# A hybrid RWKV-7 and short-convolution layer on one core: new layouts for values and decays, one more buffer for the inverse, PSUM banks shared out differently, output weights loaded in steps

## The chip, the cores and the metric

The kernel runs on one core of one Trainium2 chip, as one program. The core has five engines with their own instruction queues: TensorE (PE in the profile; PEld is its loading of weights), VectorE (DVE), ScalarE (ACT), GpSimd (POOL) and SyncE (SP), which here does nothing but issue DMAs. The metric is the device time of one execution in microseconds (us); lower is better. Three runs of the kernel before took 1731.84, 1737.47 and 1740.01 us, so its time is given as the median, 1737.47 us.

## The reference

One inference step of a one-layer backbone over 128 context tokens and 2048 latent tokens of width 1024. Cut to what matters:

```python
h = rmsnorm(x) * (1 + scale) + shift            # scale, shift from c @ w_ada
r, k, v, g_a, b_gate, c_gate, u, g_b = split(h @ w_in)      # 8 x 512 columns
r, k, v = token_shift(r, k, v)                  # mix with both neighbours
w = exp(-exp(-softplus(-(w0 + tanh(h @ dd) @ du)) - 0.5))   # decay, per direction
a = sigmoid(ib + (h @ idn) @ iu)                            # per direction
# per direction and head (8 heads of 64), over the tokens in scan order:
S = S * w_t - (S kk_t) (kk_t * a_t)^T + v_t k_t^T ;  y_t = S r_t
ya = (groupnorm(y_fwd + y_bwd) * gn_w + gn_b + bonus * v) * silu(g_a)
yb = b_gate * conv3(c_gate * u) * silu(g_b)
out = rmsnorm(x + gate * (concat(ya, yb) @ w_out)) * final_g
```

The context is scanned from a zero state and its final states are an output; the latent scans start from cached states.

## The kernel before

All data are float32, and products that need the precision are made from a high and a low part. There are three phases, written as Python generators that are advanced in turns. Between phases data pass through scratch tensors in HBM (`S[...]`, shapes in `SCR`, L686).

**Phase 1** (`phase1`, L49) works on blocks of 384 tokens (`BLK`, six of them, the last 256) in three thirds of two blocks. For each of four head pairs `g` it runs `mixA` (keys, receptance, decays, rates; L350) for both blocks of the third and then `gateA` (values and gate; L424), with the convolution group (`convB`, `gateB`) between. `dense` (L153) makes each projection from 24 matmuls.
- In `mixA`, for each direction `d`, `pt` holds exp of the cumulated log decay of each chunk of 64 tokens. It has one buffer for each direction (`NPP = 1`, L296). One element for each chunk, the whole chunk's decay, is stored by a DMA that ScalarE issues (L404): 48 DMAs, with a row of 6 (or 4) separate elements for each of 128 partitions. Phase 2 loads them as `B.pc` (L764).
- In `gateA`, `vt` holds the transposed, mean-free values with tokens on the partitions, and one DMA of SP stores it (L444) to `S["vt"]`, which is (token, 512). In the first third `vt` has one buffer under the tag "vt", which the low parts `hsl...` of `part_sum` (L200, L195, subtraction on POOL at L197) use too.

**Phase 2** (`phase2`, L704) works on 17 stages; 16 of them hold 8 chunks of one head pair in both directions, and stage 15 holds the context. The parts of a stage are: `partL` loads operands, `partM` makes within-chunk matrices F, GA and Q on TensorE (L905, L898; PSUM pool `pm` with 2 banks, L718) and sends the small diagonal blocks to HBM, `partI` inverts these on POOL (L932 to L948; tile `zt` with 2 buffers), `partW`, `partU` and `partB` load and combine, and `partS` (L1047) does the scan: 8 steps, in each step two heads' matmuls for each of the two directions into `psS` (PSUM pool `pS`, 4 banks, L752), then the next state from `psS` on VectorE (L1080). One `psS` tile holds four steps of one direction. After the fourth, `outputs` (L1088) takes it out of PSUM: a copy on ScalarE for the direction that comes first to a block of tokens (L1099, done at L792), an add on VectorE (L1097) for the other. `load_v` (L832) loads the values into `sv`: for each of 64 partitions 8 pieces of 128 elements; for the context in two DMAs.

The parts run ahead of one another: in stage s the scan of s is interleaved with `partM` of s + 3, and with `partW`, `partU` and `partB` of s + 1, by the strings `ORDER` and `MORD`. What is emitted in this order is then laid out by the framework's scheduler (`schedule_with_timeline_sim=True`, L1422), which orders each engine's instructions by its own model of times; each engine then works strictly through its list. So the order on an engine is close to, but not, the order of the source.

**Phase 3** (`phase3`, L1265) is the output projection, 17 tiles of 128 tokens. From stage 14 on phase 2's pools `pm`, `r2` and `r1` are closed and `weights` (L1306) loads the four blocks of output weights for the convolution half (`load_k`, L1276: a DMA, a copy on ScalarE to the high part, a subtraction on VectorE to the low part; `raw` has 2 buffers), all before the scan of stage 14 is emitted. `ahead` (L1314) then makes the convolution half of three tiles, a half tile for each step of the scan; `tail` does the rest after stage 16.

Of the kernel before, what the change touches and what calls it, by code (L numbers as in the profile page):

```python
# [6 lines left out]
F32 = mybir.dt.float32  # L7
F32R = mybir.dt.float32r
# [3 lines left out]
PSUM = bass.MemoryType.PSUM  # L12
DRAM = bass.MemoryType.DRAM

NT = 2176
# [33 lines left out]
def phase1(K):  # L49
# [285 lines left out]

    npair = [0]
# [13 lines left out]
    def mixA(g, j, ws, hh, lw, pre):  # L350

        t0, n = BLK[j]
        nch = n // 64
        tl = lambda tag, b=1: (tp if tag == "sg" else ta_).tile([128, 384], F32, tag=tag, name=f"{tag}_{g}_{j}_{K.u()}", bufs=b)
# [16 lines left out]
        for d in range(2):  # L371
# [32 lines left out]
            nc.scalar.dma_start(S[f"pc{d}"][g * 128:(g + 1) * 128, t0 // 64:t0 // 64 + nch], pt[:, :nch, 64 - 64 * d])  # L404
# [10 lines left out]
            kds.append(kd)  # L415
        bs = kds[0]
# [7 lines left out]
    def gateA(g, j, ws, hh, bsum):  # L424

        t0, n = BLK[j]
        tl = lambda tag, b=1: (tp if tag == "sg" else ta_).tile([128, 384], F32, tag=tag, name=f"{tag}_{g}_{j}_{K.u()}", bufs=b)
# [16 lines left out]
        nc.sync.dma_start(S["vt"][t0:t0 + n, g * 128:(g + 1) * 128].rearrange("(a p) c -> p a c", p=128), vt[:, :n // 128])  # L444
# [241 lines left out]
SCR = {}  # L686
for _d in range(2):
    SCR[f"ops{_d}"] = (4, 512, NT)
    SCR[f"pc{_d}"] = (512, 34)
SCR.update(vt=(NT, 512), sg=(512, NT), q=(512, NT), mixT=(1024, NT))  # L690
# [13 lines left out]
def phase2(K):  # L704
# [8 lines left out]
    def setup_first():  # L713
# [4 lines left out]
        O.pm = Pool(K, "p2m", "right", 2, PSUM)  # L718
# [29 lines left out]
    def setup_rest():  # L748
# [3 lines left out]
        O.pS = Pool(K, "p2S", "left", 4, PSUM)  # L752
# [10 lines left out]
        for d in range(2):  # L763
            D(B.pc[:, d], S[f"pc{d}"].rearrange("(e c) n -> c e n", c=64))  # L764
# [67 lines left out]
    def load_v(dst, units):  # L832
        if units[0][0] == units[-1][0]:
            p, c0 = units[0]
            D(dst.rearrange("t u h v -> t u (h v)"), S["vt"][c0 * 64:(c0 + 8) * 64, p * 128:(p + 1) * 128].rearrange("(u t) c -> t u c", t=64))
        else:
            for u in range(2):
                D(dst.rearrange("t (g u) h v -> t u g (h v)", u=2)[:, u], S["vt"][u * 64:u * 64 + 64, :].rearrange("t (g c) -> t g c", g=4))
# [83 lines left out]
    def partI(s, st):  # L922
# [5 lines left out]
        zt = tl([128, 16, 32], "zt", 2, O.rI)  # L928
# [336 lines left out]
def phase3(K):  # L1265
# [10 lines left out]
    def load_k(k, hi, lo, eng):  # L1276

        raw = O.r.tile([128, 1024], F32, tag="raw", name=f"woraw{k}", bufs=2)
        D(raw[:], A["wout"][k * 128:(k + 1) * 128, :])
        P.copy(hi[:], raw[:])  # L1280
# [25 lines left out]
    def weights():  # L1306
# [3 lines left out]
        for k in CONV:  # L1310
            load_k(k, *[O.r.tile([128, 1024], F32R, name=f"wo{a}{k}") for a in "hl"], V)
        z0[AHEAD[0]] = O.r.tile([128, 1024], F32, name="z0_0")

    def ahead():  # L1314
        for i in AHEAD:
# [111 lines left out]
```

## Time and profile before

| | |
|---|---|
| median of 3 runs | 1737.47 us (1731.84 to 1740.01) |
| the profiled execution | 1726.64 us, of which the span from first to last instruction is 1724.9 us |
| instructions | 32848 |
| stages of phase 2 by the first and last scan matmul | stage 0 from 1017.3 us, stage 14 from 1456.1, stage 15 from 1480.0, stage 16 from 1528.4 to 1561.0 us |
| mean granted TensorE clock | 0.970 |

The profiled execution is 10.8 us, or 0.6%, shorter than the median. In the rows, "PE psF L905 <- ACT Q L792: 9.4, 17, 1.6" reads: the matmuls of line 905 that write tile psF waited for the instruction of ScalarE that writes Q, 9.4 us in total, 17 times, at longest 1.6 us. A row of a timeline has the start and the duration in us, the engine, the line, the operation, output <- inputs with their shapes, how many instructions are merged in the row, and in brackets the engine's idle time before it with what ended it. A row of the windows view has, for each engine, its busy time and its number of instructions, then the granted TensorE clock (1.00 is full), the DMA engines' busy share and GB/s.

### The profile page before, as it was taken

The page shows a single profiled execution, that of the slowest core. Times are in us where ns is not written, and L with a number is a line of the kernel's source. Part 1 is how long each engine was busy: PE and PEld are TensorE (multiplying, and loading weights), DVE is VectorE, ACT ScalarE, POOL GpSimd, SP SyncE. Part 2 cuts the span into 40 slices and gives each one's busy share as a digit, 9 for nine tenths or more (in the row PEclk, how much of TensorE's full clock was granted, in tenths as well). Part 3 has the DMA queues.
Part 4 walks back from the last instruction along what each step waited for, and adds up shares of the span by engine and source line. Part 5 has one row for each costly group of instructions (what it writes and reads, how often), then busy time and mean ns, then how long its engine had stood idle before and what let it go on. Part 6 is the DMA issues. An engine that isn't in the chain of part 4 may idle for free. (4 is left out here: it accounts for less than half of the span.)

```text
span 1724.9 us, 32848 instructions
## 1 busy us (share of the span) xinstructions
PE 1640.9 (95%) x12400; PEld 1556.2 (90%) x12400; DVE 1107.3 (64%) x2092; ACT 868.8 (50%) x1719; POOL 587.4 (34%) x1089
## 2 busy tenths in 40 slices
PE   5989899999999999999999989999999999999998
PEld 2889889899999999999999989999999999887886
DVE  5875778775568858587854344666766656646433
ACT  4533454443243534244423187788878777643222
POOL 0010111111110201021213737877877768223221
PEclk8899999999999999999999999899999989899999
DMA  9687778675557657567896376677878874746442
GB/s 372 212 221 235 223 245 252 199 234 183 173 182 209 176 173 188 167 188 248 208 304 218 112 191 154 163 185 186 203 186 189 189 177 106 195 153 202 147 147 92
DMA packets 314286, 335.66 MB, mean 195 GB/s; under 512 B 165448, under 2 KB 262344, under 8 KB 300048
## 3 DMA queue, kind: packets, MB, share of 16 engines
q1 hardware_dynamic: 277184, 328.97, 65.3%
q10 hardware_dynamic: 35584, 0.14, 1.3%
q0 software_dynamic: 1360, 4.46, 0.7%
q8 instruction: 98, 1.61, 0.4%
q14 instruction: 60, 0.49, 0.1%
HBM read 221.42 MB, written 112.08 MB: 193 GB/s over the span
## 5 line engine op out<-in xcount | busy, mean ns | idle before, releaser
L947 POOL TENSOR_TENSOR zt<-zt,ztmp 128x30 f32<-128x30 f32 (+7 forms) x510 | 198.6, 389 | 39.3
L1067 PE MATMUL psS<-sv,E 128*128 128x64 f32 x1088 | 154.4, 277 | 0.0
L1067 PEld LDWEIGHTS psS<-sv,E 128*128 128x128 f32 x1088 | 145.4, 200 | 1.9
L1042 PE MATMUL psE<-str,stl 128*128 128x128 f32 x1088 | 140.8, 278 | 5.4 <-DVE E L1043 3.8
L944 POOL TENSOR_TENSOR ztmp<-ab,zt 128x60 f32<-128x60 f32 (+7 forms) x255 | 133.5, 524 | 19.4
L1042 PEld LDWEIGHTS psE<-str,stl 128*128 128x128 f32 x1088 | 129.8, 192 | 7.1 <-DVE E L1043 4.8
L323 POOL TENSOR_TENSOR shk<-rawl 128x384 f32<-128x384 f32 (+1 forms) x24 | 23.0, 959 | 322.6 <-ACT rawl L319 322.6
L1080 DVE TENSOR_TENSOR sv<-psS,pc 64x128 f32<-64x128 f32 x254 | 69.4, 277 | 97.3 <-PE psS L1067 96.9
L792 ACT COPY bd<-rr 64x512 f32<-64x512 f32 x136 | 84.0, 617 | 77.2 <-issue 24.5
L1043 DVE TENSOR_TENSOR E<-psE,msk 128x512 f32<-128x512 f32 x136 | 92.9, 685 | 27.6 <-PE psE L1042 26.9
L905 PE MATMUL psF<-rr,bd 128*128 128x128 f32 x544 | 78.8, 291 | 13.0 <-ACT Q L792 10.6
L1363 POOL TENSOR_TENSOR z<-z,x 128x512 f32<-128x512 f32 x32 | 43.6, 1364 | 126.5 <-DVE z L1359 105.8
L905 PEld LDWEIGHTS psF<-rr,bd 128*128 128x128 f32 x544 | 69.2, 199 | 16.3 <-ACT Q L792 13.1
L1031 PE MATMUL psX<-F,zb 128*128 128x128 f32 x544 | 80.7, 303 | 2.7 <-ACT zb L790 1.7
L323 POOL TENSOR_TENSOR shv<-rawl 128x384 f32<-128x384 f32 (+1 forms) x24 | 22.3, 930 | 178.2 <-ACT rawl L319 172.9
L905 PE MATMUL psG<-rr,bd 128*128 128x128 f32 x544 | 74.8, 286 | 2.9 <-DVE F L906 2.9
L1031 PEld LDWEIGHTS psX<-F,zb 128*128 128x128 f32 x544 | 73.7, 214 | 3.6 <-ACT zb L790 2.4
L160 PE MATMUL mmc<-h,w 128*128 128x384 f32 (+1 forms) x192 | 66.7, 347 | 6.8 <-ACT ta L397 3.4
L905 PEld LDWEIGHTS psG<-rr,bd 128*128 128x128 f32 x544 | 68.2, 199 | 3.3 <-DVE F L906 3.0
L161 PE MATMUL mmc<-h,w 128*128 128x384 f32 (+1 forms) x192 | 65.5, 341 | 0.0
L162 PE MATMUL mmc<-h,w 128*128 128x384 f32 (+1 forms) x192 | 65.4, 340 | 0.0
L160 PE MATMUL mmgb<-h,w 128*128 128x384 f32 (+1 forms) x192 | 64.4, 335 | 0.4 <-ACT q1r L321 0.4
(307 smaller groups left out, 5177.2 us busy)
## 6 DMA issues: line engine op xcount, KB each, us to landing
w<-scr_wsp SPq DMA_DIRECT2D x68, 1024.0 KB, 6.7
scr_wsp<-w SPq DMA_DIRECT2D x34, 1024.0 KB, 9.0
rr<-scr_ops SPq DMA_DIRECT2D x64, 512.0 KB, 4.4
scr_ops<-pair SPq DMA_DIRECT2D x80, 384.0 KB, 6.7
wr<-in_win SPq DMA_DIRECT2D x34, 512.0 KB, 6.1
ab<-scr_at SPq DMA_DIRECT2D x34, 256.0 KB, 3.8
x<-in_x SPq DMA_DIRECT2D x17, 512.0 KB, 3.7
wadas<-in_wada SPq DMA_DIRECT2D x8, 1024.0 KB, 14.1
```

The lines of the kernel that those rows point to most:

```text
L160: T.matmul(ps[:, :n], w[:, 0, k], hh[:, 0, k, :n], start=k == 0, stop=False)
L161: T.matmul(ps[:, :n], w[:, 0, k], hh[:, 1, k, :n], start=False, stop=False)
L162: T.matmul(ps[:, :n], w[:, 1, k], hh[:, 0, k, :n], start=False, stop=k == 7)
L792: (V.tensor_copy if k in ON_DVE else P.copy)(dst, src)
L905: T.matmul(ps[:, i, :].rearrange("p (a b) -> p a b", b=64), w[:, u, :], x[:, :, u, :], start=True, stop=True)
L944: G.tensor_tensor(tv, ab[:, j:j + 2, j + 2:32].unsqueeze(1).broadcast_to((128, kn, 2, n)), zt[:, :kn, j:j + 2].unsqueeze(3).broadcast_to(( ...
L947: G.tensor_tensor(zt[:, :kn, j + 2:32], zt[:, :kn, j + 2:32], tv[:, :, r], ALU.subtract)
L1031: T.matmul(px[:, i, :], B.zb[:, gi, us.start + i, :], g.F[:, us.start + i, :], start=True, stop=True)
L1042: T.matmul(pe[:, i, hd, :].rearrange("p (b t) -> p b t", b=2), g.lt[:, :, hd, us.start + k + i].rearrange("p b t -> p (b t)"), g.rt[:, :, ...
L1043: V.tensor_tensor(g.E[n][:, k:k + 2].rearrange("p a b c -> p (a b) c"), pe[:].rearrange("p a b c -> p (a b) c"), B.msk[:, ME[g.d]].unsquee ...
L1067: T.matmul(sp[gi][:, q, hd, :], g.E[n][:, k, hd, :], sv[:, u, hd, :], start=True, stop=True)
L1080: r = V.tensor_tensor(dst, sp[gi][0:64, q], B.pc[0:64, d, 2 * p:2 * p + 2, c:c + 1].broadcast_to((64, 2, 64)), ALU.mult)
```

## The change

Five edits:
- The values' scratch tensor becomes (4 head pairs, 64 tokens, 34 chunks, 128). A store becomes two DMAs, one for the even and one for the odd chunks, each from 64 partitions; a load takes 8 chunks that lie together (one piece of 1024 elements for each partition), and the context's load becomes one DMA.
- The chunk decays of both directions and both blocks of a third are gathered by a POOL copy into a tile `pcs`, and stored by one DMA of SP after the second block: 12 DMAs instead of 48 of ScalarE.
- `zt` gets a third buffer.
- PSUM pool `pm` gets 3 banks in place of 2 and `pS` 3 in place of 4.
- `weights` only starts the loading of the first two weight blocks. The copies and subtractions, and the loading of the other two, become steps of `ahead`, one block at each step of the scan, so that the convolution halves come five steps later.

```diff
@@ -333,6 +333,7 @@
         t0, n = BLK[j]
         nc.sync.dma_start(S[name][g * 128:(g + 1) * 128, t0:t0 + n], t_[:, :n])
 
+    pcsum = {}
     npair = [0]
 
     def pair():
@@ -351,6 +352,10 @@
 
         t0, n = BLK[j]
         nch = n // 64
+        c0, pc0 = t0 // 64, BLK[j - j % 2][0] // 64
+        if j % 2 == 0:
+            pcsum[g] = tp.tile([128, 2, 12], F32, tag="pcs", name=f"pcs{g}_{j}", bufs=2)
+        pcs = pcsum[g]
         tl = lambda tag, b=1: (tp if tag == "sg" else ta_).tile([128, 384], F32, tag=tag, name=f"{tag}_{g}_{j}_{K.u()}", bufs=b)
         wk, wr_ = ws
         psk, psr = pre or (None, None)
@@ -401,7 +406,7 @@
             V.tensor_tensor(v3(al), v3(kk), pt[:, :nch, d:64 + d], ALU.mult)
             V.tensor_tensor(v3(rh), v3(rS), pt[:, :nch, 1 - d:65 - d], ALU.mult)
             spill2(d, 2 * d, g, j, ar)
-            nc.scalar.dma_start(S[f"pc{d}"][g * 128:(g + 1) * 128, t0 // 64:t0 // 64 + nch], pt[:, :nch, 64 - 64 * d])
+            G.tensor_copy(pcs[:, d, c0 - pc0:c0 - pc0 + nch], pt[:, :nch, 64 - 64 * d])
 
             kd = tl("kd", 2)
             P.activation(kd[:, :n], ta[:, :n], AF.Identity, bias=dcol(D_KA2 + g), scale=vcol(V_KA + g))
@@ -413,6 +418,8 @@
             V.tensor_tensor(be[:, :n], be[:, :n], c[:, :n], ALU.mult)
             spill2(d, 2 - 2 * d, g, j, kb)
             kds.append(kd)
+        if j % 2:
+            nc.sync.dma_start(S["pc"][g * 128:(g + 1) * 128, :, pc0:c0 + nch], pcs[:, :, :c0 + nch - pc0])
         bs = kds[0]
         V.tensor_tensor(bs[:, :n], kds[0][:, :n], kds[1][:, :n], ALU.add)
         V.scalar_tensor_tensor(bs[:, :n], bs[:, :n], dcol(D_RKQ + g), rS[:, :n], ALU.mult, ALU.mult)
@@ -424,6 +431,7 @@
     def gateA(g, j, ws, hh, bsum):
 
         t0, n = BLK[j]
+        nch = n // 64
         tl = lambda tag, b=1: (tp if tag == "sg" else ta_).tile([128, 384], F32, tag=tag, name=f"{tag}_{g}_{j}_{K.u()}", bufs=b)
         wv, wg = ws
         vS = shifted(dense(wv, hh, n, "v"), j, 2, g, "v", 1)
@@ -441,7 +449,8 @@
         mn = ta_.tile([128, 3, 2], F32, tag="vmean", name=f"vmean{g}_{j}", bufs=1)
         V.tensor_reduce(mn[:, :m], heads(psv), mybir.AxisListType.X, ALU.add)
         V.scalar_tensor_tensor(heads(vt), mn[:, :m].unsqueeze(3).broadcast_to((128, m, 2, 64)), -1.0 / 64, heads(psv), ALU.mult, ALU.add)
-        nc.sync.dma_start(S["vt"][t0:t0 + n, g * 128:(g + 1) * 128].rearrange("(a p) c -> p a c", p=128), vt[:, :n // 128])
+        for i in range(2):
+            nc.sync.dma_start(S["vt"][g, :, t0 // 64 + i:t0 // 64 + nch:2], vt[i * 64:i * 64 + 64, :nch // 2])
 
         psg = dense(wg, hh, n, "g")
         tg = tl("sg", 2)
@@ -686,8 +695,7 @@
 SCR = {}
 for _d in range(2):
     SCR[f"ops{_d}"] = (4, 512, NT)
-    SCR[f"pc{_d}"] = (512, 34)
-SCR.update(vt=(NT, 512), sg=(512, NT), q=(512, NT), mixT=(1024, NT))
+SCR.update(pc=(512, 2, 34), vt=(4, 64, 34, 128), sg=(512, NT), q=(512, NT), mixT=(1024, NT))
 
 
 
@@ -715,7 +723,7 @@
         O.r0 = Pool(K, "p2r0", "right")
         O.rI = Pool(K, "p2rI", "right")
         O.r1 = Pool(K, "p2r1", "right")
-        O.pm = Pool(K, "p2m", "right", 2, PSUM)
+        O.pm = Pool(K, "p2m", "right", 3, PSUM)
         B.msk = O.r0.tile([128, 4, 128], F32, name="msk")
         B.mkg = O.r0.tile([128, 2, 128], F32, name="mkg")
         for i, j in enumerate((0, 2, 4, 5)):
@@ -749,7 +757,7 @@
         O.l0 = Pool(K, "p2l0", "left")
         O.l1 = Pool(K, "p2l1", "left")
         O.p2 = Pool(K, "p2s", "left", 2, PSUM)
-        O.pS = Pool(K, "p2S", "left", 4, PSUM)
+        O.pS = Pool(K, "p2S", "left", 3, PSUM)
         O.r2 = Pool(K, "p2r2", "right")
         new_slot(O.r2)
         cp = O.l0
@@ -761,7 +769,7 @@
         V.memset(B.geps[:], 64e-5)
         B.pc = cp.tile([64, 2, 8, 34], F32, name="pc")
         for d in range(2):
-            D(B.pc[:, d], S[f"pc{d}"].rearrange("(e c) n -> c e n", c=64))
+            D(B.pc[:, d], S["pc"][:, d].rearrange("(e c) n -> c e n", c=64))
 
         lt = ring(O.l1, 2, [128, 2, 8, 128], "stl", lambda t_: presetS(vl(t_)))
         rt = ring(O.l1, 2, [128, 2, 2, 8, 64], "str", presetS)
@@ -832,10 +840,9 @@
     def load_v(dst, units):
         if units[0][0] == units[-1][0]:
             p, c0 = units[0]
-            D(dst.rearrange("t u h v -> t u (h v)"), S["vt"][c0 * 64:(c0 + 8) * 64, p * 128:(p + 1) * 128].rearrange("(u t) c -> t u c", t=64))
+            D(dst.rearrange("t u h v -> t u (h v)"), S["vt"][p, :, c0:c0 + 8])
         else:
-            for u in range(2):
-                D(dst.rearrange("t (g u) h v -> t u g (h v)", u=2)[:, u], S["vt"][u * 64:u * 64 + 64, :].rearrange("t (g c) -> t g c", g=4))
+            D(dst.rearrange("t (g u) h v -> t g (u h v)", u=2), S["vt"][:, :, 0:2].rearrange("g t u c -> t g (u c)"))
 
     H0, H1, FULL = slice(0, 64), slice(64, 128), slice(0, 128)
 
@@ -925,7 +932,7 @@
         ab = tl([128, 32, 32], "ab", 2, O.rI)
         for h in range(2):
             D(ab[h * 64:h * 64 + 64].rearrange("p j i -> p (j i)"), at.rearrange("u s b j i -> (u s b) (j i)"))
-        zt = tl([128, 16, 32], "zt", 2, O.rI)
+        zt = tl([128, 16, 32], "zt", 3, O.rI)
         zf = zt[:].rearrange("p a b -> p (a b)")
         tmp = tl([128, 512], "ztmp", 1, O.rI)
         dg = tl([128, 16], "dgp", 1, O.rI)
@@ -1273,10 +1280,15 @@
     AHEAD = TILES[:3]
     z0 = {}
 
-    def load_k(k, hi, lo, eng):
+    def load_raw(k):
 
         raw = O.r.tile([128, 1024], F32, tag="raw", name=f"woraw{k}", bufs=2)
         D(raw[:], A["wout"][k * 128:(k + 1) * 128, :])
+        return raw
+
+    def load_k(k, hi, lo, eng, raw=None):
+
+        raw = raw or load_raw(k)
         P.copy(hi[:], raw[:])
         eng.tensor_tensor(lo[:], raw[:], hi[:].bitcast(F32), ALU.subtract)
         wk[k] = (hi, lo)
@@ -1307,11 +1319,16 @@
         O.r = Pool(K, "p3r", "right")
         O.pr = Pool(K, "p3pr", "right", 2, PSUM)
         O.pu = O.pr
-        for k in CONV:
-            load_k(k, *[O.r.tile([128, 1024], F32R, name=f"wo{a}{k}") for a in "hl"], V)
+        O.raw = [load_raw(k) for k in CONV[:2]]
         z0[AHEAD[0]] = O.r.tile([128, 1024], F32, name="z0_0")
 
     def ahead():
+        yield
+        for n, k in enumerate(CONV):
+            load_k(k, *[O.r.tile([128, 1024], F32R, name=f"wo{a}{k}") for a in "hl"], V, O.raw[n])
+            if n < 2:
+                O.raw.append(load_raw(CONV[n + 2]))
+            yield
         for i in AHEAD:
             ms = load_m(O.r, i, CONV, 1)
             if i not in z0:
```

## The prediction

> **What bounds the kernel now.** I read the page first, then a windows view cut at the phases, then TensorE's waits by stretch, and last timelines around single waits.
>
> ```profile
> PE 1640.9 (95%) x12400; PEld 1556.2 (90%) x12400; DVE 1107.3 (64%) x2092; ACT 868.8 (50%) x1719; POOL 587.4 (34%) x1089
> ```
>
> TensorE is busy for 95% of the span, and no other engine comes near. An edit here is worth what it takes from TensorE's idle time or gives to it, and idle time of other engines does not count by itself. Where the idle time lies (columns: us, then busy us and instructions of PE, PEld, DVE, ACT, POOL, then clock, DMA share, GB/s):
>
> ```profile
> 0.00:150.00 150.00, 122.86 (x627) 103.09 (x627) 106.69 (x209) 62.82 (x118) 11.79 (x25) 0.92 0.81 261
> 150.00:975.00 825.00, 802.82 (x4841) 789.17 (x4840) 573.89 (x1042) 334.63 (x677) 151.46 (x201) 0.99 0.70 208
> 975.00:1017.00 42.00, 34.83 (x347) 33.05 (x346) 16.38 (x34) 22.95 (x46) 14.26 (x29) 0.88 0.64 154
> 1017.00:1476.00 459.00, 445.24 (x5322) 434.19 (x5320) 284.84 (x588) 362.96 (x696) 350.78 (x786) 0.96 0.71 171
> 1476.00:1528.00 52.00, 47.55 (x395) 42.28 (x395) 29.90 (x56) 32.55 (x58) 10.80 (x15) 0.90 0.71 193
> ```
>
> TensorE is idle for 27 us in the start-up, which no edit touches; 22 us in the rest of phase 1; 7 us between the phases; 14 us in fifteen stages of the scan; and 4.5 us where the output weights come in. There is a second loss: a clock of 0.96 over 459 us is 18 us of work. Its form is stretches at half clock, such as these two; the row of TensorE is the wait right ahead of the second:
>
> ```profile
> 1378.55 1.82 PE L905 MATMUL psF<-rr,bd 128*128 128x128 f32 x8 [1.63 <-ACT Q L792]
> 1099.00:1109.20 10.20, 10.20 (x100) 9.73 (x101) 1.72 (x5) 3.99 (x7) 6.42 (x17) 0.50 0.41 126
> 1378.90:1389.10 10.20, 10.20 (x103) 9.73 (x102) 2.88 (x6) 4.28 (x8) 7.71 (x19) 0.50 0.64 174
> ```
>
> So what all edits together could win at most is about 22 + 7 + 14 + 4.5 = 48 us of idle time and 18 us of clock. What TensorE waited for in phase 1, and then in the scan, says how much of that they reach:
>
> ```profile
> PE pss L204 <- ACT hshs L196: 5.5, 3, 3.0
> PE pss L205 <- POOL hsls L197: 3.3, 2, 2.6
> PE mmc L160 <- ACT q1r L321: 2.9, 4, 2.0
> PE psq L205 <- POOL hslq L197: 1.7, 1, 1.7
> ```
>
> ```profile
> PE psF L905 <- ACT Q L792: 9.4, 17, 1.6
> PE psW L1012 <- ACT bu L792: 1.5, 4, 0.5
> ```
>
> **Decays in 12 stores.** Removed are 48 issues on ScalarE; added are 48 copies on POOL, which I price by the nearest row, POOL's copy of 128x16, and 12 issues on SP, priced like a value store below.
>
> ```profile
> L404 ACTq DMA_DIRECT2D scr_pc<-pp x48: 366/366/1160, 80.9 to 864.9; - x48
> 1202.12 0.21 POOL L936 COPY dgp<-ab 128x16 f32<-128x16 f32 x1
> q10 hardware_dynamic: 35584, 0.14, 1.3%
> ```
>
> ScalarE gets back 48 x 0.366 = 17.6 us in phase 1. It is busy for 335 of 825 us there, and what delays TensorE through it (5.5 + 2.9 us above) are instructions that ScalarE itself got late from VectorE. At best all 8.4 us go; I take 1. POOL gets 48 x 0.21 = 10 us, and is busy for 151 of 825 us. The copy waits for the exp of `pt`. What is queued behind it on POOL are the shift additions and the low parts, and these wait for ScalarE instructions that stand behind that exp anyway. So the wait adds nothing and the copy lies in idle time; without that cover TensorE, which waits for POOL's low parts, pays 0.21 us at each of the 3 places above, under 1 us. The 35584 packets of 4 bytes that go were 1.3% of the DMA engines' span; loads of weights gain a little, which the rows don't carry to TensorE. Term: -1 us (-8.4 to +1).
>
> **Values by head pair.** There are 24 more stores on SP, and lighter loads.
>
> ```profile
> L444 SPq DMA_DIRECT2D scr_vt<-vt x24: 359/371/1010, 131.7 to 885.6; - x24
> POOL hslq L197 <- DMA scr_vt<-vt: 25.8, 2, 16.4
> scr_vt<-vt SPq DMA_DIRECT2D x20, 192.0 KB, 4.1
> sv<-scr_vt SPq DMA_DIRECT2D x32, 256.0 KB, 4.0
> ```
>
> The issues cost SP 24 x 0.37 = 9 us and the decay stores 12 x 0.37 = 4.4 us, spread over 750 us; queued behind them are loads and stores that wait for engines anyway. The landing matters in the first third, where the low parts use the same buffer: POOL waited 25.8 us there, though TensorE behind it only 1.7 us. If the second half lands 0.37 us later than the one store did, the two waits of that row pass on under 1 us: I take +0.5. If the second half only starts when the first has landed, it is 4.1 us later, and two waits give +8.
>
> [...]
>
> The loads lose nothing by longer pieces, and no wait of TensorE on `sv` stands in the rows, so a gain there is hidden. Term: +0.5 us (0 to +8).
>
> **Third place for the inverse.**
>
> ```profile
> POOL zt L932 <- DMA scr_zt<-zt: 20.7, 6, 4.7
> ```
>
> The memset for the next inverse is laid ahead of the current one's first copy, and waits until the store that POOL issued just before has landed. With three buffers six such waits, 20.7 us of POOL, can go, unless the scheduler pulls the memset ahead by one more. But POOL is busy for 351 of 459 us, and TensorE waits on POOL nowhere in the scan. Term: 0. The inverse is covered by the two stages between it and its use; without that cover a wait would cost its own 3.5 us.
>
> **PSUM 3 and 3.** Here two waits of the same kind trade places. Stage 8, with the two directions' copies on ScalarE, and then stage 10, with adds on VectorE instead:
>
> ```profile
> 1282.75 1.10 PE L1067 MATMUL psS<-sv,E 128*128 128x64 f32 x8
> 1285.26 0.38 PE L905 MATMUL psF<-rr,bd 128*128 128x128 f32 x1 [1.40 <-ACT Q L792]
> 1284.01 0.58 ACT L792 COPY y<-psS 64x512 f32<-64x512 f32 x1
> ...
> 1347.02 1.16 PE L905 MATMUL psF<-rr,bd 128*128 128x128 f32 x8 [1.26 <-ACT Q L792]
> 1348.11 0.24 PE L1012 MATMUL psW<-zc,bu 32*32 32x32 f32 x2
> 1346.99 1.18 ACT L792 COPY bu<-psU 32x512 f32<-32x512 f32 x2
> ```
>
> With two `pm` banks the second psF needs the bank that Q is copied from. With three it needs that of the last GA, which is free long before: this wait goes. But with three `pS` banks the second direction's fifth step takes the bank that the first direction's copy y has to leave. In stage 8 that copy ends at 1284.59 us, and the second half of the psS row, from about 1283.3, has to wait for it. TensorE then comes to psF at about 1285.3, as it does now: nothing is won. In stage 10 the add is done in time and psF can start 1.26 us sooner, but psW is next, and needs bu, whose two copies run on ScalarE to 1348.17 in either case. The first of them ends at about 1347.58, so psW could start 0.5 us sooner than 1348.11. What is late next is ScalarE, which runs without a gap there. So of 9.4 us I take 3.
>
> Between the phases one stage's F, GA and Q are made with little beside them, and there TensorE waited as follows:
>
> ```profile
> PE psG L905 <- DVE F L906: 2.9, 1, 2.9
> PE psF L905 <- ACT Q L792: 1.2, 1, 1.2
> ```
>
> A third bank takes these two, 4.1 us; I take half, 2. For `pS` there are eight places where the copy ends after the matmuls that would need its bank. Here are the first, in stage 1, and the last and worst, in the context's stage:
>
> ```profile
> 1065.12 0.56 PE L1067 MATMUL psS<-sv,E 128*128 128x64 f32 x4
> 1066.15 1.19 ACT L792 COPY y<-psS 64x512 f32<-64x512 f32 x2
> ```
>
> ```profile
> 1496.53 0.56 PE L1067 MATMUL psS<-sv,E 128*128 128x64 f32 x4
> 1501.46 0.58 ACT L792 COPY y<-psS 64x512 f32<-64x512 f32 x1
> ```
>
> As the lists stand, the first would wait from 1065.12 to 1066.74, where the first of the two copies ends, 1.6 us, and the last until 1502.04, 5.5 us. The scheduler knows of the new wait and has the convolution's matmuls to put first, so I take +1.5 (0 to +5.5). Term: -3 - 2 + 1.5 = -3.5 us (-13.5 to +12).
>
> **Output weights in steps.**
>
> ```profile
> 1479.37 1.04 ACT L1280 CAST woh<-woraw 128x1024 fp32r<-128x1024 f32 x1 [1.97 <-DMA woraw<-in_wout]
> 1480.44 1.23 DVE L1281 TENSOR_TENSOR wol<-woraw,woh 128x1024 fp32r<-128x1024 f32 x1 [1.49 <-ACT woh L1280]
> 1482.33 0.94 PE L1042 MATMUL psE<-str,stl 128*128 128x128 f32 x6 [1.76 <-DVE E L1043]
> ```
>
> The chain is: ScalarE stands 1.97 us before a weight that has not landed, VectorE then 1.49 us, and TensorE 1.76 us behind VectorE. Emitted step by step, the copies may be laid behind the scan's own work. But the first two loads are emitted where they were, and the copy runs when its load lands; so of the 4.5 us idle time in 1476 to 1528 I take 2. The convolution halves come later in the list, and if they miss the gaps of the context's stage, up to 2 us are lost. Term: -2 us (-4.5 to +2).
>
> **Sum.** -1 + 0.5 + 0 - 3.5 - 2 = -6.0 us. The profiled execution of 1726.6 us would become 1720.6. It was 10.8 us under the median, and I take the same difference for the kernel after: 1737.5 - 6.0 = 1731.5 us, 0.35% below. About 0.5%, 8.7 us, is what a measurement of this kernel can tell from no change, so the forecast is no change, on the faster side.
>
> **Rivals.**
> *The waits on Q go and the half-clock stretches with them.* For it: 10.6 us (9.4 + 1.2) of such waits, and the stretch above starts right behind one; each of the two costs half of 10.2 us. That gives 10.6 + 10.2 = 20.8 us and 1716.7 us. Against it: the copy bu is next. [...] Chance of a gain over 0.5% by this way: 0.37.
>
> *The scan waits for its outputs.* With three `pS` banks ScalarE's copy y decides whenever it ends after TensorE has come to the second direction's fifth step. In the lists as they stand those are the eight places: stage 1 with 1.6 us, stage 8 with 1.3, five more with less, and the context's with 5.5. At an estimated 0.9 us for each of the first seven and 5.5 for the last this is 11.8 us; if the third `pm` bank gives nothing back, the time is 1737.5 + 11.8 = 1749.3 us. Against it: where ScalarE is late, psF waits now. Chance: 0.18.
>
> *The edits change nothing that TensorE waits for*: the memset is pulled ahead again and the weights' copies stay together. That gives 1737.5 us, and is part of the no-change case, 0.45.
>
> **How the numbers follow.** The forecast and the third rival make no change, 0.45; the first is faster, 0.37; the second slower, 0.18. The range reaches to the first rival's 1716.7 and, on the other side, most of the way to the second's 1749.3, since the vt bound of +8 leads there too: 1716 to 1746.
>
> **What would show it.** Right: psF's waits on Q are nearly gone; psS now waits on ScalarE's y in stages 1, 4, 5, 8, 9, 12, 13 and 15; psW waits more on bu; ScalarE's busy time in phase 1 is the same with 48 issues fewer; POOL's waits on the zt store are gone and TensorE doesn't notice. Wrong: the scan from 1017 us to the end of stage 14 shorter by more than 10 us, or granted clock in it at 0.98 or more (first rival); waits of psS on y over 8 us in total (second); or a change of over 5 us in phase 1, which I hold to be indifferent.

## The result, and the profile after

The kernel after takes 1689.16 us (median of 4 runs, 1687.23 to 1694.44), the kernel before beside it on the same chip 1734.65 us (1731.49 to 1740.01). The ratio is 0.9739, with a 95% interval of 0.9703 to 0.9776: 45.5 us faster, where 6 were forecast and the range ended at 1716. The profiled execution of after takes 1689.68 us (span 1687.9), about its median; that of before lies 8 us under its own, so that the two traces show 37 of the 45.5 us.

TensorE's line on the page of after, and then its windows view, cut at the same work as the rows of before (the phases' ends lie at 951 and 993 us now, the same point of stage 14 at 1439):

```profile
PE 1620.6 (96%) x12400; PEld 1540.7 (91%) x12400; DVE 1111.2 (66%) x2092; ACT 869.0 (51%) x1719; POOL 621.8 (37%) x1137
```

```profile
0.00:150.00 150.00, 128.20 (x665) 109.20 (x666) 108.43 (x212) 65.56 (x124) 15.86 (x30) 0.97 0.77 276
150.00:951.00 801.00, 789.96 (x4802) 778.21 (x4801) 574.70 (x1039) 332.50 (x672) 190.91 (x262) 1.00 0.61 212
951.00:993.00 42.00, 34.37 (x369) 33.00 (x368) 18.02 (x36) 24.17 (x48) 5.73 (x13) 0.96 0.72 166
993.00:1439.00 446.00, 434.37 (x5310) 425.72 (x5309) 287.29 (x591) 362.40 (x695) 356.19 (x796) 0.97 0.73 178
1439.00:1491.00 52.00, 45.98 (x384) 40.68 (x385) 26.20 (x49) 30.85 (x55) 4.78 (x2) 0.90 0.61 163
```

Phase 1 ends 24 us earlier (975 to 951), the way to the scan is as long as before, the scan up to that point of stage 14 is 13 us shorter (459 to 446), and the end is unchanged. Phase 1 was to be indifferent. A finer cut finds the place. These are the windows of before and of after for the rest of the first third and for the middle of phase 1; the windows of each kernel hold the same work, by the number of matmuls:

```profile
150.00:404.00 254.00, 241.16 (x1334) 230.96 (x1333) 188.81 (x342) 118.24 (x222) 32.58 (x32) 0.99 0.77 234
404.00:830.00 426.00, 421.03 (x2542) 418.84 (x2542) 301.78 (x540) 174.74 (x368) 68.11 (x71) 1.00 0.64 188
```

```profile
150.00:385.10 235.10, 231.01 (x1293) 222.46 (x1292) 188.55 (x339) 115.75 (x217) 48.93 (x43) 0.99 0.68 244
385.10:811.00 425.90, 420.91 (x2541) 418.59 (x2540) 301.75 (x542) 174.74 (x368) 81.32 (x99) 1.00 0.55 188
```

From 404 to 830 us nothing changed, 426.0 against 425.9 us, though 28 of the 48 decay stores lie there. Of the 24 us, 19 were won ahead of that and 5 behind it (830 to 975 us against 811 to 951). Of the 19, 14.1 us are idle time of TensorE: 5.3 in the first 150 us (its busy time there is 128.2 against 122.9) and 8.8 up to 404 us (254.0 less 241.2 is 12.8; 235.1 less 231.0 is 4.1). So it is not the instructions that were saved, but something that above all the first third waits for. The waits view (us in total, times, longest) has it, of before and then of after:

```profile
ACT w L125 <- DMA wr<-in_win: 30.6, 10, 10.1
DVE pair L401 <- DMA scr_ops<-pair: 30.1, 10, 4.9
```

```profile
ACT w L125 <- DMA wr<-in_win: 7.9, 6, 3.7
DVE pair L406 <- DMA scr_ops<-pair: 6.0, 1, 6.0
```

VectorE makes the operands of the scan in tiles `pair` and may write one again when the DMA that stored it has landed. In the first third there are two such tiles; later two more, under the tag "wr", are used in turn with them (`pair`, L341 to L348). Of the 30.1 us, 29.2 lie in the first third. The DMA issues (KB each, median us to landing), before and after, show what the wait is made of:

```profile
scr_wsp<-w SPq DMA_DIRECT2D x34, 1024.0 KB, 9.0
scr_ops<-pair SPq DMA_DIRECT2D x80, 384.0 KB, 6.7
scr_pc<-pp ACTq DMA_DIRECT2D x40, 3.0 KB, 9.1
```

```profile
scr_wsp<-w SPq DMA_DIRECT2D x34, 1024.0 KB, 4.9
scr_ops<-pair SPq DMA_DIRECT2D x80, 384.0 KB, 3.8
```

The same stores of the same size land in 3.8 us instead of 6.7. What went is beside them: decay stores of 3 KB that took 9.1 us each.

In the scan, these are TensorE's waits of after from 993 to 1417.5 us, which is stages 0 to 13, up to the first matmul of stage 14, and the windows row of that stretch; the row of before, cut at the same work, stands behind it:

```profile
PE psW L1019 <- ACT bu L800: 4.2, 4, 1.7
PE psF L912 <- DMA rr<-scr_ops: 1.7, 1, 1.7
PE psE L1049 <- ACT stl L798: 1.5, 1, 1.5
```

```profile
993.00:1417.50 424.50, 414.50 (x5034) 406.56 (x5034) 274.80 (x562) 346.68 (x664) 340.56 (x758) 0.97 0.75 181
```

```profile
1017.30:1456.10 438.80, 425.12 (x5054) 414.53 (x5053) 273.83 (x563) 348.24 (x666) 336.07 (x754) 0.96 0.73 175
```

The 9.4 us of psF on Q are gone, psW waits 2.7 us more on `bu`, as forecast, and psS on y nowhere. Of the 14.3 us, idle time has 3.7 (438.8 less 425.1 against 424.5 less 414.5) and TensorE's busy time 10.6. Part of the latter is clock: cut into pieces of 3.4 us, these stages lose 17.1 us to a clock below full before and 12.0 us after. The other 5.5 us of busy time no row explains; the row of after has 20 matmuls fewer, an estimated 1.7 us of it at the mean of 84 ns (425.1 us for 5054).

### The profile page after: what moved, and what is told of

Its sections match the earlier page's. It is cut to its first block, busy times and chain, and to the rows that moved or that the text cites. A ratio compares the mean times of both kernels' runs of the same rounds, so it can differ in the third digit from the quotient of the medians.

```text
span 1687.9 us, 32921 instructions
## 1 busy us (share of the span) xinstructions
PE 1620.6 (96%) x12400; PEld 1540.7 (91%) x12400; DVE 1111.2 (66%) x2092; ACT 869.0 (51%) x1719; POOL 621.8 (37%) x1137
## 5 line engine op out<-in xcount | busy, mean ns | idle before, releaser
L1049 PE MATMUL psE<-str,stl 128*128 128x128 f32 x1088 | 151.1, 286 | 9.7 <-ACT str L798 5.0
L1049 PEld LDWEIGHTS psE<-str,stl 128*128 128x128 f32 x1088 | 136.7, 199 | 11.5 <-ACT str L798 5.7
L409 POOL COPY pcs<-pp 128x6 f32<-128x6 f32 (+1 forms) x48 | 28.2, 588 | 130.8 <-ACT pp L398 130.8
L1038 PE MATMUL psX<-F,zb 128*128 128x128 f32 x544 | 72.8, 283 | 0.3 <-ACT zb L798 0.3
L323 POOL TENSOR_TENSOR shv<-rawl 128x384 f32<-128x384 f32 (+1 forms) x24 | 24.6, 1024 | 129.4 <-ACT rawl L319 126.3
L1038 PEld LDWEIGHTS psX<-F,zb 128*128 128x128 f32 x544 | 67.2, 198 | 0.5 <-issue 0.5
L160 PE MATMUL mmc<-h,w 128*128 128x384 f32 (+1 forms) x192 | 64.3, 335 | 3.4 <-ACT q1r L321 2.9
L913 DVE TENSOR_TENSOR GA<-psG,mkg 128x512 f32<-128x512 f32 x68 | 46.8, 690 | 31.4 <-PE psG L912 26.2
```

The costliest lines, as they stand in the source:

```text
L160: T.matmul(ps[:, :n], w[:, 0, k], hh[:, 0, k, :n], start=k == 0, stop=False)
L1038: T.matmul(px[:, i, :], B.zb[:, gi, us.start + i, :], g.F[:, us.start + i, :], start=True, stop=True)
L1049: T.matmul(pe[:, i, hd, :].rearrange("p (b t) -> p b t", b=2), g.lt[:, :, hd, us.start + k + i].rearrange("p b t -> p (b t)"), g.rt[:, :, ...
```

## The experiments

Theory A, formed on these rows: pieces of 4 bytes in the decay stores hold up the DMAs beside them, and the first third waits for those. Rivals: ScalarE's 48 issues (17.6 us); the number of stores; `pt` coming free earlier, since a copy reads it and no DMA. For the scan the question is which half of the PSUM split gains. The 17 kernels, with the median and ratio to the kernel before, which ran beside each, and, of the profiled execution, VectorE's wait on the pair stores at L401 (its line in the kernels with `pcs` is L406) and the start of the scan, which is the end of phase 1 and the way to the scan:

| run | kernel | median us | ratio (95%) | pair wait | scan from us |
|---|---|---|---|---|---|
| e1_pc | before + gathered decays | 1703.42 | 0.983 (0.977 to 0.989) | 6.0 | 992.3 |
| e2_psum | before + PSUM 3 and 3 | 1722.70 | 0.994 (0.991 to 0.996) | | 1021.6 |
| e3_vt_zt_w | before + the three other edits | 1734.90 | 1.001 (0.998 to 1.004) | | 1023.4 |
| e4_sp4 | before, decay stores issued by SP | 1735.66 | 1.001 (0.998 to 1.004) | 37.5 | 1021.1 |
| e5_pc48 | gathered, 48 stores of 24-byte pieces | 1706.26 | 0.982 (0.978 to 0.985) | 7.0 | 994.4 |
| e6_pc4B | e1 + 24 stores of 4-byte pieces | 1805.71 | 1.040 (1.037 to 1.043) | 47.3 | 1086.3 |
| e7_double | before, each decay store twice | 1811.00 | 1.042 (1.039 to 1.046) | 67.3 | 1093.3 |
| e8_pS3 | before, pS 3, one bank idle | 1738.55 | 1.001 (0.998 to 1.003) | | 1024.1 |
| e9_p2s3 | after, pS 2, p2 3 | 1702.90 | 0.979 (0.974 to 0.984) | | 995.2 |
| e10_pc_psum | before + gathered decays + PSUM 3 and 3 | 1691.29 | 0.973 (0.968 to 0.978) | | 990.9 |
| e11_pc64B | e1 + 48 stores, 64-byte pieces | 1706.00 | 0.983 (0.978 to 0.988) | 6.5 | 992.6 |
| e12_pc8B | e1 + 48 stores, 4-byte pieces 8 apart | 1727.09 | 0.994 (0.991 to 0.997) | 30.7 | 1014.9 |
| e13_pc16B | e1 + 48 stores, 16-byte pieces | 1722.66 | 0.992 (0.990 to 0.995) | 26.3 | 1012.0 |
| e14_burst | e1 + 24 stores, 4-byte pieces side by side | 1810.02 | 1.043 (1.039 to 1.046) | 51.5 | 1097.0 |
| e15_pc32B | e1 + 48 stores, 32-byte pieces | 1706.48 | 0.981 (0.977 to 0.985) | 6.3 | 995.5 |
| e16_pc64Boff | e11, pieces begin 32 bytes into a row | 1709.78 | 0.981 (0.975 to 0.987) | 6.2 | 997.2 |
| e17_pc64Boff16 | e11, pieces begin 16 bytes into a row | 1714.39 | 0.988 (0.983 to 0.994) | 8.0 | 998.9 |

The extra stores of e6, e7 and e11 to e17 go to a scratch tensor `pcx` that nothing reads; all kernels compute everything. In e11 to e13 and e15 to e17 there are 34816 pieces of the named size, as many as the kernel before stores in its decays. In the kernel before the scan begins at 1017.3 us, after at 993.0.

**Which edit (e1, e2, e3).** Each is a part of the change's diff, alone: the hunks of `pcs` and `S["pc"]`; the two PSUM lines; the hunks of `vt`, `zt` and the weights.

> The kernel before with the gathered decays alone (POOL copies, 12 stores by SP). Theory: in phase 1 the 34816 four-byte packets of the decay stores held up the other DMAs, above all the stores of the pair buffers for which VectorE waited 30.1 us in the kernel before, and this edit alone gives the 18 to 24 us that phase 1 became shorter: 1710 to 1718 us, scr_ops<-pair landing in about 3.8 us instead of 6.7, and VectorE's wait on it under 10 us. Rival: phase 1's gain comes from other edits or from the scheduler's new order; then this run is within 8 us of the kernel before and the landing times stay at 6 to 7 us.

> The kernel before with PSUM 3 and 3 alone. Theory: the scan's 14 us (stage 0 to stage 14 took 438.8 us before and 424.5 after) come from the third pm bank, so this run is at 1717 to 1724 us with phase 1 unchanged (stage 0 starts at 1017 us, plus or minus 3). Rival as the prediction had it: the wait moves to bu or to the psS banks, and the time changes by under 5 us.

> The kernel before with the three other edits: values by head pair, third place for the inverse, output weights in steps. Theory: these hardly matter, 1729 to 1737 us. Rival: one of them gives the scan's gain (shorter value loads or the inverse's free place), then stage 0 to stage 14 is 10 us or more shorter than 438.8 us.

The medians differ from before's 1735.81 by -32.4, -13.1 and -0.9 us; their sum, -46.4, is as large as the whole, -45.5. e1 lies 7 us under the range of its theory, which came from two traces: in that of before the scan begins at 1017.3 us, in those of e2, e3, e4 and e8, with the same decay stores, at 1021.1 to 1024.1. The gathered decays gain in phase 1 alone: in e1 the scan begins at 992.3 us, and its stages 0 to 13 take 438.7 us, where before takes 438.8. The PSUM split gains in the scan alone. The windows rows of those stages, of e1 and of e2:

```profile
992.30:1431.00 438.70, 425.80 (x5054) 415.49 (x5053) 273.99 (x564) 348.27 (x666) 333.86 (x754) 0.96 0.75 175
```

```profile
1021.60:1446.70 425.10, 415.19 (x5035) 407.05 (x5034) 272.59 (x561) 346.70 (x664) 338.30 (x751) 0.97 0.77 180
```

In the traces with three `pm` banks (after, e2, e9, e10) these stages take 421.7 to 426.1 us, in all the others 438.3 to 448.9.

**What of the decay stores (e4 to e7).** e4 moves the 48 issues to SP, e5 gathers but stores every block and direction by itself, e6 adds the same number of 4-byte pieces again to e1, e7 doubles the stores of before (shortened, `...` stands for what is left out):

```diff
e4  -  nc.scalar.dma_start(S[f"pc{d}"][...], pt[:, :nch, 64 - 64 * d])
e4  +  nc.sync.dma_start(S[f"pc{d}"][...], pt[:, :nch, 64 - 64 * d])
e5  +  nc.sync.dma_start(S["pc"][g * 128:(g + 1) * 128, d, c0:c0 + nch], pcs[:, d, c0 - pc0:c0 - pc0 + nch])
e5  -  if j % 2: nc.sync.dma_start(S["pc"]...)
e6  +  for d in range(2):
e6  +      nc.sync.dma_start(S["pcx"][g * 128:(g + 1) * 128, pc0:c0 + nch, d], pcs[:, d, :c0 + nch - pc0])
e7  +  nc.scalar.dma_start(S[f"pcx{d}"][...], pt[:, :nch, 64 - 64 * d])
```

> The kernel before, with the 48 decay stores issued by SP instead of ScalarE, four-byte packets as before. If the packets are the cost, this stays within 6 us of the kernel before and scr_ops<-pair still lands in 6 to 7 us. If ScalarE's 17.6 us of issuing were the cost, it gains most of phase 1's 18 to 24 us.

> As the gathered decays alone, but each POOL copy is stored by its own DMA of SP, 48 stores with pieces of 24 bytes instead of 12 stores. Theory: what cost time was the number of single four-byte pieces, 34816, not the number of stores; here they are 6144, so nearly all of the gain stays: 1702 to 1710 us, with scr_ops<-pair landing in about 4 us. Rival: the number of stores counts; then it falls back by half or more, to 1718 us or above.

> The gathered decays, and beside their 12 stores 24 more that write the same values once more to a scratch tensor that nobody reads, in four-byte pieces: 34816 such packets come back, but pt is still released by POOL's copy, ScalarE issues nothing and the sources are gathered. Theory of the packets: phase 1 is as slow as in the kernel before, 1725 to 1740 us, and scr_ops<-pair lands in 6 to 7 us. Rival, that the earlier release of pt or the gathering made the gain: under 1710 us.

> The kernel before with every decay store made twice by ScalarE, the second time to a scratch tensor that nobody reads: twice the four-byte packets. Theory: the cost comes a second time, 12 to 30 us over the kernel before, 1748 to 1766 us, and scr_ops<-pair lands in 9 us or more. If the packets are harmless: within 6 us of the kernel before.

With ScalarE free of the issues nothing is won (e4); with 48 stores of whole rows, in 6144 pieces, all is won (e5); with `pt` free and the small pieces back everything is lost, and more (e6); with twice as many the loss is 74.0 us (e7). e6 and e7 lie far over the ranges of their theories, and in e7 ScalarE also waits 16.1 us for the extra stores before it may write `pt` again, so not all of its loss need come of what the pieces do to other stores. The three rivals fall: the issues by e4, the number of stores by e5, and `pt` by e6 and, more cleanly, by e11 and e15 below, where 48 stores read `pt` as before and the gain stays. Two rows of the waits view of e4, the same waits as before, and then three of the DMA view of e6:

```profile
DVE pair L401 <- DMA scr_ops<-pair: 37.5, 11, 6.1
ACT w L125 <- DMA wr<-in_win: 31.7, 11, 9.9
```

```profile
scr_ops<-pair SPq DMA_DIRECT2D x80, 384.0 KB, 4.0
scr_ops<-pair SPq DMA_DIRECT2D x16, 256.0 KB, 14.2
scr_pcx<-pcs SPq DMA_DIRECT2D x16, 6.0 KB, 16.7
```

A store of 6 KB that takes 16.7 us is what such pieces look like on a page. In e6 the pair stores of 384 KB land in 4.0 us, not in the 6 to 7 that its theory expected: the extra stores come only once for two blocks, so the median hides them, and VectorE's 47.3 us are five waits, the longest of 17.9 us.

**How small is small (e11, e13, e15), and where (e12, e16, e17).** To e1 is added, at the place of before's stores:

```diff
+  nc.sync.dma_start(S["pcx"][g * 128:(g + 1) * 128, c0:c0 + nch, d, :], pt[:, :nch, 24:40])   # e11; e13 24:28, e15 24:32
+  nc.sync.dma_start(S["pcx"][..., d], pt[:, :nch, 64 - 64 * d])                # e12, pcx (512, 34, 2)
+  nc.sync.dma_start(S["pcx"][..., d, 8:24], pt[:, :nch, 24:40])                # e16, pcx (512, 34, 2, 32); e17 4:20
```

> Gathered decays, and 48 more stores on SP of 64-byte pieces from pt to a scratch that nothing reads: as many packets as the kernel before has (34816 more than with gathered decays alone), at the same places, 16 times the bytes. Theory (the count of packets delays what is behind them, not how small they are): as with the 4-byte pieces on SP, 1730 to 1745 us, DVE's wait on the pair stores 30 to 40 us. Rival (a write under some size is dear by itself, and 64 bytes are above it): 1703 to 1712 us, DVE's wait on the pair stores 6 to 12 us.

> Gathered decays, and 48 more stores on SP of 4-byte pieces from pt to a scratch that nothing reads, laid there 8 bytes apart, not side by side. The run with 24 extra stores whose pieces lay 8 bytes apart cost 102 us more than the gathered decays alone, though as many packets side by side, as before has them, cost 32. Theory A (it is where the pieces land: pieces that do not lie side by side are dearer): 1790 to 1810 us. Theory B (it was the size of the single burst, 24 stores of 1408 packets instead of 48 of 704): 1730 to 1745 us, as with 48 stores side by side on SP.

> Gathered decays, and 48 more stores on SP from pt to a scratch that nothing reads, in pieces of 16 bytes, otherwise as the run with 64-byte pieces (1706 us) and the one with 4-byte pieces 8 bytes apart (1727 us). Theory (what is dear is a 4-byte piece, a packet with a single element): 1702 to 1710 us, DVE's wait on the pair stores under 12 us. Rival (the cost goes with how far a piece is below 64 bytes): 1716 to 1727 us, DVE's wait on the pair stores 20 to 31 us.

> Gathered decays, and 48 more stores on SP from pt to a scratch that nothing reads, in pieces of 32 bytes. Pieces of 4 bytes gave 1727 us, of 16 bytes 1723, of 64 bytes 1706, no such stores 1703. Theory (a piece that does not fill a block of 64 bytes is dear, however large a part of it): 1718 to 1728 us, DVE's first wait on the pair stores 20 to 31 us. Rival (half a block is already enough): 1702 to 1710 us, that wait under 12 us.

> Gathered decays, and 48 more stores on SP from pt to a scratch that nothing reads, in pieces of 64 bytes that each lie across two blocks of 64 bytes (32 bytes into a row of 128). Theory (a block that is written in part is dear: two of them for each piece): 1718 to 1745 us, DVE's first wait on the pair stores over 20 us. Rival (only the length of a piece counts): 1702 to 1712 us, as with 64-byte pieces that fill a block.

> Gathered decays, and 48 more stores on SP from pt to a scratch that nothing reads, in pieces of 64 bytes that begin 16 bytes into a row of 128. Theory (a block of 32 bytes that is written in part is what costs; each piece now has two of them, where a 16-byte piece had one): 1718 to 1750 us, DVE's wait on the pair stores over 20 us. [...] Rival (only a piece's length counts): 1702 to 1712 us, that wait under 12 us.

My theory of e11 fell: the count of packets by itself cost nothing here. As many packets with 64 bytes, 16 times the data, give 1706 us and the pair stores land in 4.1 us, where e1 has 1703 us and 3.6. That of e13 fell too: 16 bytes are as dear as 4 (1723 us against 1727). With 32 bytes the cost is gone (1706 us); there the theory fell a third time, that a block of 64 must be filled. The DMA rows of e13 and of e15:

```profile
scr_ops<-pair SPq DMA_DIRECT2D x80, 384.0 KB, 6.0
scr_pcx<-pp SPq DMA_DIRECT2D x40, 12.0 KB, 4.5
```

```profile
scr_ops<-pair SPq DMA_DIRECT2D x80, 384.0 KB, 4.3
scr_pcx<-pp SPq DMA_DIRECT2D x40, 24.0 KB, 2.0
```

Twice the bytes land in less than half the time. Whether both ends must lie on a multiple of 32 bytes stays half open: e17, with neither end there, lies at 1714 us between the two answers, and outside both expectations; its pair stores land in 5.1 us. Its interval overlaps that of e16 (1709.8 us). In its trace the scan begins 6.6 us later than in e1, in that of e16 4.9; the rest of e17's time lies behind that, where no extra store runs. So the length decides most, and the place of the ends less than that: counted from the kernel before beside each, 16-byte pieces cost 18 us more than 32-byte ones (e13, e15), 64-byte pieces that begin 32 bytes into a row 5 us more than those of e11 (e16), and 16 bytes into it 11 us (e17). Why the step lies between 16 bytes and 32 no run shows.

**Why 24 stores cost more than 48 (e14).** Each counted from the kernel before beside it (e1: -32.4 us), e6 lost 101 us against e1, e12 only 20 with as many packets. That is also less than the 32 us that before's own decay stores cost; where the other 12 come from isn't shown. e14 is e6 with `pcs` interleaved, (12, 2), and with it `S["pc"]` and `B.pc`, so that the extra pieces land side by side:

```diff
+  nc.sync.dma_start(S["pcx"][g * 128:(g + 1) * 128, d, pc0:c0 + nch], pcs[:, :c0 + nch - pc0, d])   # pcx (512, 2, 34)
```

> Gathered decays with the two directions interleaved in the buffer, and 24 more stores on SP of 4-byte pieces from it, issued in pairs as in the run that cost 102 us, but landing side by side. Theory (the size of the burst: up to 1536 small packets per store and two stores in a row, which all later stores and loads queue behind): 1780 to 1810 us, landing of the extra stores 14 to 18 us. Rival (in that run it was the two interleaved stores landing between each other's pieces at the same time): 1720 to 1745 us, landing under 10 us.

It loses as much (1810.0 us, the extra stores land in 18.5, both just over the theory's ranges), so it isn't where the pieces land. What e6 and e14 share is the burst: two stores of up to 1536 small pieces in a row, where e12 has single ones of up to 768 with VectorE's work between them; e12's 1727 us lies 3 us under the range of its theory B. The waits view and the DMA view of e14:

```profile
DVE pair L406 <- DMA scr_ops<-pair: 51.5, 4, 19.9
```

```profile
scr_pcx<-pcs SPq DMA_DIRECT2D x16, 6.0 KB, 18.5
```

Four waits, the longest of 19.9 us. The size of a store and the pairing weren't tried apart.

**The PSUM split (e8, e9), and the rest (e10).** e8 and e9 change only the numbers of banks: `"p2S"` 4 to 3 in the kernel before; `"p2S"` 3 to 2 and `"p2s"` 2 to 3 in the kernel after. e10 has the edits of e1 and e2.

> The kernel before with the psS pool cut from 4 to 3 banks and nothing in exchange; one bank lies idle. As the prediction priced it, the copies y that end too late cost 5 to 12 us here, 1741 to 1748 us. Theory after the first runs: the scheduler lays the y copies earlier, the cut costs nearly nothing, 1733 to 1738 us, and the whole gain of PSUM 3 and 3 is the third pm bank's.

> The kernel after, with one bank moved on from the scan's outputs: pm 3, pS 2, p2 3 instead of pm 3, pS 3, p2 2. Theory (the scan gains where the maker of F, GA and Q need not wait for the copy of Q, and nothing in it waits for an output's bank): taking one more bank from the outputs costs little, but now each step takes the bank that the step before last left, whose copy y ends 1 to 3 us after its matmuls; half of these wait for some 0.3 us, 136 steps x 0.15 = 20 us dearer, and p2's third bank wins back a few of the waits on E: 1689 + 5 to 20, so 1694 to 1710. Rival (the banks of outputs never bind, the scheduler moves the copies): 1680 to 1692.

> The kernel before with two of the five edits, the gathered decays and the PSUM split, and without the values' layout, the third place and the weights in steps. Theory (these two are the whole gain): ratio to before 0.974, 1687 to 1693 us, within 0.4% of the kernel after. Rival (the three others only win together with these two, when TensorE has less to hide them behind): 1695 to 1705 us.

Two rows of TensorE's waits in e8:

```profile
PE psF L905 <- ACT Q L792: 8.3, 17, 1.4
...
PE psS L1067 <- ACT y L792: 3.1, 6, 1.9
```

With three banks for outputs and no third one for `pm` the waits of psS on y exist, 3.1 us at 6 places, and the median is 1.6 us longer (interval -2.8 to +4.9), half a microsecond over the range of its theory. So the gain is the third `pm` bank's, but the reason in that theory is wrong: without that bank the copies of y don't come earlier. ScalarE's list in e8 is that of before in all but 14 of 1755 places, and in both kernels 16 of 34 copies of y end more than 3 us behind the matmuls of the fourth step. With the third `pm` bank ScalarE's list differs in 664 places (e2), only 7 of the 34 end so late, in e2 and in after alike, and the waits of psS on y are gone.

A split still further (e9) is 11.6 us slower than e10 on the same chip, within its theory's range; the two intervals overlap. The cause put into that expectation is not shown: e9's profile, of the quickest of its four executions, has no wait of psS on ScalarE's y, and its stages 0 to 13 take 421.7 us, less than the 424.5 of after. What is longer is the part from stage 14 to the end, 276.4 us against 270.4. e10 equals the kernel after: the three other edits are worth nothing beside these two either, and no version is faster clear of noise.

## Why the prediction was wrong

**Decays, -1 us (-8.4 to +1): -32.4.** This is the failed step, and it is "The 35584 packets of 4 bytes that go were 1.3% of the DMA engines' span; loads of weights gain a little, which the rows don't carry to TensorE". I priced small packets by the time that they themselves take, and their effect on others at nothing. Two rows of before speak against it, and the working uses neither: VectorE's 30.1 us on the pair stores, and the landing of 9.1 us for a store of 3 KB. In the first third the chain is VectorE on the pair stores, ScalarE and POOL on VectorE, TensorE on these: the waits on `hshs`, `hsls` and `hslq` that the prediction quotes, 10.5 us, are 1.2 us in e1. The prediction says that ScalarE got those instructions late from VectorE, and doesn't ask what VectorE had waited for. The bound of 8.4 us was the sum of two waits in rows of TensorE, of which that on `q1r` stayed (3.1 us in e1), while TensorE was idle for 12.8 us from 150 to 404 us, and for 27 in the start-up "which no edit touches": after, the first 150 us hold 5.3 us more of its work. POOL's copies were under-priced as well. The groups of after have them at 588 ns, not 210; ScalarE waited for one of them, 1.7 us, and TensorE for none. Why they are slower stays open: their source elements lie 260 bytes apart, but those of the copy that I took the price from lie 264 bytes apart too (L936 reads every 66th element):

```profile
L409 POOL COPY pcs<-pp 128x6 f32<-128x6 f32 (+1 forms) x48 | 28.2, 588 | 130.8 <-ACT pp L398 130.8
```

**Values, +0.5 (0 to +8), inverse 0, weights -2 (-4.5 to +2): together -0.9 in e3** (interval -4.0 to +6.2). The +8, for a second half that only starts when the first has landed, is not to be seen: e3's interval ends at +6.2, and POOL waits 25.8 us at 2 places on the store in e3, as before. Half stores of e3 and of after, and whole stores of e10:

```profile
scr_vt<-vt SPq DMA_DIRECT2D x40, 96.0 KB, 3.1
scr_vt<-vt SPq DMA_DIRECT2D x40, 96.0 KB, 2.3
scr_vt<-vt SPq DMA_DIRECT2D x20, 192.0 KB, 2.2
```

Beside gathered decays (after, e10) a half takes as long as a whole, and in the four pairs of which the trace of after has both landings the second half lands 0.2 to 0.6 us behind the first; the 4.1 us of which the +8 was made no run shows. The loads in longer pieces lose nothing, as forecast: 3.9 us to landing in e3, 4.0 before. The wait on the zt store is 13.8 us after, at 7 places, from 20.7 at 6, but the kernels with two places for zt have 12.7 (e7) to 21.1 (e14), so this is no clear drop: three memsets are laid ahead of the first copy now and two before, as I had allowed, and TensorE doesn't notice. The weights' gain isn't there: in the 52 us where they come in, TensorE is idle for 6.0 us (52.0 less 45.98) instead of 4.5.

**PSUM, -3.5 (-13.5 to +12): -13.1.** The mechanism was that of the first rival, and right in kind: the waits on Q go, and part of the lost clock with them (5.1 us by the pieces above, where the rival had 10.2). What failed is "nothing is won" in stage 8, worked out with the lists "as they stand": with the third `pm` bank the scheduler laid ScalarE's list anew and the copies of y came earlier. The +1.5 for psS also fell away in the kernel after. In e8, where the list did stay nearly as it stood, it is about right: 3.1 us of waits where the rival that ends slower had 11.8, and 1.6 us in the median. That rival is thereby refuted in the kernel after.

**The clock.** The waits on Q alone, 9.4 us in the scan and 1.2 between the phases, are 10.6 us; with the half-clock stretches, by the first rival, 20.8. e2 won 13.1, nearer to the waits alone. The scan of after still has stretches at half clock, three of 6.8 us and one of 3.4, though the waits on Q are gone and TensorE's longest wait there is 1.7 us, so those waits can't be what brings on all of them; what does, no run shows. In the four traces with three `pm` banks, stages 0 to 13 lose 8.5 to 15.4 us to the clock, in the 15 with two 13.7 to 23.9. The clock's part is an argument from the traces; no run was made for it.

**The end.** Of the signs named for "wrong", two came: the scan shorter by more than 10 us, and a change of over 5 us in phase 1.

## What to carry to other kernels

Price a store by what waits beside it: a DMA whose KB are few and whose landing takes long (here 3 KB, 9.1 us) is a warning, and then the waits on landings of all engines are to be read, VectorE's too, above all where a tile has only two places (29.2 of VectorE's 30.1 us here). Gather single elements on chip until the pieces that land in HBM have at least 32 bytes (34816 extra pieces cost 19 us at 16 bytes and 1 at 32), and spread small ones rather than issue them in a burst (20 us in 48 single stores of 4-byte pieces, 101 in 24 issued in pairs). When a resource is moved between two uses, the scheduler may lay its lists anew (as for the third `pm` bank) or hardly at all (as for the cut of `pS` alone), so a wait worked out in the old lists is not a forecast until the new lists have been looked at.

## What the runs showed of the hardware that was not expected

- The small packets themselves are not slow in the records: in phase 1 the 4-byte ones take 10 ns in the mean before, the 16-byte ones 8.5 in e13, the 64-byte ones 9.7 in e11. What shows of the delay is in the large packets beside them: the 1536-byte packets, most of them the pair stores', take 86 ns in the mean before and 67 after, and 1 in 100 takes over 558 ns before and over 119 after (worked out from the packets' records in the traces). At an estimated 16 packets of a pair store for each of 16 engines (384 KB in packets of 1536 bytes, over the page's 16 DMA engines), the 19 ns are only 0.3 of the 2.9 us that the store lands later; how much the rare slow packets, or waits between packets, make of the rest is not shown. So the share of the DMA engines' time, 1.3%, says nothing of the cost.
- The cost is a step in the size of a piece: for 34816 extra pieces 20 us at 4 bytes, 19 at 16, 1 at 32 and -1 at 64 (e12, e13, e15 and e11, less e1, each counted from the kernel before beside it).
- It depends on how they come: the same number in pairs of large stores costs 101 to 106 us (e6, e14), and twice the number of before's 74 us more (e7, with ScalarE's waits for `pt` in it).
- ScalarE waits on `wr` for 24.0 us in e11 and 7.9 us after, and e11 lost nothing in phase 1 by it (its scan begins at 992.6 us, that of after at 993.0): e12, which begins it 22.6 us later than e1, has 22.8 us of that wait. So of two waits of 30 us in the kernel before, the time goes with VectorE's. A third tile for `pair` in the first third, which would show that path directly, wasn't tried.
